# Four modulation blocks of the second layer computed between the layers, with the weights as the held operand

## The chip, the cores and the metric

The kernel runs on one core of one Trainium2 chip. The metric is the device time of one execution in microseconds; a lower time is better. Five engines work side by side, each through its own instructions in order, and wait for each other by semaphores: TensorE (PE, matrix products, with its weight loads listed apart as PEld), VectorE (DVE), ScalarE (ACT), GpSimd (POOL) and SyncE (SP, which here issues the transfers from and to DRAM).

## What is computed

A two-layer backbone over 512 latent tokens on an 8 x 64 grid and 256 context tokens, width 1024. Every sub-layer stands between a modulated RMS norm and a gated residual; shifts, scales and gates come from a small product of the conditioning vectors with a large matrix, per layer:

```python
for layer in range(DEPTH):
    mod_l = jnp.split((jax.nn.silu(c) @ w_mod[layer] + b_mod[layer])[:, None, :], 6, axis=-1)
    mod_c = jnp.split((jax.nn.silu(c_ctx) @ w_mod[layer] + b_mod[layer])[None, None, :], 6, axis=-1)
    hl = modulate(rmsnorm(xl, norm_g[layer, 0]), mod_l[0], mod_l[1])
    hc = modulate(rmsnorm(xc, norm_g[layer, 0]), mod_c[0], mod_c[1])
    ...  # layer 0: mLSTM and GLA heads; layer 1: RWKV-7 time mixing
    xl = xl + mod_l[2] * rmsnorm(yl, norm_g[layer, 1])
    hl = modulate(rmsnorm(xl, norm_g[layer, 2]), mod_l[3], mod_l[4])
    xl = xl + mod_l[5] * rmsnorm(conv_ffn(hl, ...), norm_g[layer, 3])
```

The change concerns `silu(c) @ w_mod[1]` and `silu(c_ctx) @ w_mod[1]`: two rows of 1024 times a matrix of 1024 x 6144. Only its first third (shift and scale of the first norm) is needed before the second layer's mixer; the gate `mod[2]` and what follows are needed after its recurrence.

## The kernel before, in words

Channels lie on partitions, eight groups of 128, tokens along the free axis: context first (256, `CTX`), then the latents (512, `LAT`), which the norms treat in two halves (`H0`, `H1`). Most products split float32 into a rounded high part and a low part: `unit` loads a raw weight tile `wraw` on SP, ACT casts it to `whi`, and POOL or DVE subtracts to get `wlo`; `dense` or `projn` then issues three matmuls for each piece. The raw tiles come from one ring of 15 buffers, and a load waits until the buffer's last reader has finished.

The matrix of modulations is cut into 12 blocks of 512 columns per layer. For the second layer, blocks 0 to 3 are done with split weights during the first layer. Blocks 4 to 11 are done by `mod_fill`: for each block four raw tiles `wfill` of 512 KB, unsplit; eight float32 matmuls in which the conditioning (`cth`, 128 x 2) is held and 512 weight columns move, giving 2 x 512 in one PSUM bank `mfill`; a copy into `frow`; four small matmuls with `sel` that turn the row into columns; and an addition of the bias into `modT`. Each float32 matmul is two instructions in the trace.

The second layer begins in `rwkv_mixer` with a stretch between the layers. The last pass of the first layer's down projection (`passes`, tile `po`) ends with the residual and the norm of each segment. `residual` squares the result (`xc`) and adds pairs; `rstd` sums over channels by matmuls against a column of ones (`rsb<-onek,xc`), takes the reciprocal root on POOL (`rsc`), spreads it by matmuls against the identity (`rsb<-ident,rsc`) and copies it; `normj` applies it to `y`. Then `enter` runs for the segment: `shift` (the difference to a neighbour on the grid, `xx`, mostly on POOL), and `variant` (the token mix, `vt`, its high part `vh` on ACT and its low part `vl` on DVE). Once the context is done the first four groups of the "v" projection begin (`first` and `projn`, PSUM tiles `pjC` for the context and `pjL` for the latents), with weights from `in_rkv`.

After that come low-rank projections, "r" and "k", and the recurrence in 16 units. Here a recording layer sets the order: `flow` takes generators (threads) and asks at each step which one could go on first by a table of costs (`Meter`); steps that need PSUM banks ask for them (`"@1"`). `mod_fill` is the last thread in that list and puts 7.0 of that clock between its matmuls. Outside `flow`, the order on each engine is the one that the program's list scheduler makes of the code.

Of the kernel before, what the change touches and what calls it, by code (L numbers as in the profile page):

```python
# [13 lines left out]
ALU = mybir.AluOpType  # L14
# [4 lines left out]
P = 128  # L19
# [8 lines left out]
LAT = (256, 512, "L", 0)  # L28
# [26 lines left out]
def chain(*gens):  # L55
    for g in gens:
        yield from g
# [7 lines left out]
def staggered(gens):  # L65

    live = []
    for g in gens:
        live = [h for h in live if next(h, drain) is not drain]
        live += [g] if next(g, drain) is not drain else []  # L70
    while live:
        live = [h for h in live if next(h, drain) is not drain]
# [10 lines left out]
def merge(*streams):  # L83


    st = [[g, tot, 0.0] for g, tot in streams]
    while st:
        stuck = True
        for e in sorted(st, key=lambda e: e[2] / e[1]):
            try:  # L90
                c = next(e[0])
            except StopIteration:
                st.remove(e)
                stuck = False
                break
            if c is not None:
                e[2] += c
                stuck = False
                break
        assert not stuck  # L100
# [117 lines left out]
def flow(meter, threads):  # L218

    done, waiting, ready, engine = {}, {}, [], {}
    for i, (name, g) in enumerate(threads):
        ready.append((0.0, i, name, g, 0))

    def place(g):
        while hasattr(g.gi_yieldfrom, "gi_frame"):
            g = g.gi_yieldfrom
        return g.gi_code.co_name, g.gi_frame.f_lineno if g.gi_frame else 0

    def when(e):

        return max(e[0], meter.free.get(engine.get(place(e[3])), 0.0)), not e[2].startswith("rec"), e[0], e[1]
    while ready:
        e = min(ready, key=when)
        ready.remove(e)
        t, i, name, g, n = e
        if n:
            b = meter.banks(n)
            if b is None:  # L240
                waiting.setdefault("@", []).append(e)
                continue
            if b > t:
                ready.append((b, i, name, g, n))
                continue
        meter.begin()
        at = place(g)
        x = next(g, None)
        engine[at] = meter.first
        ready += waiting.pop("@", ())  # L250
        t = max(t, meter.end if x is None or x is True else meter.head)
        if x is None:
            done[name] = t
            ready += [(max(t, t2), *r) for t2, *r in waiting.pop(name, ())]
        elif isinstance(x, str) and x[0] == "@":
            ready.append((t, i, name, g, int(x[1:])))
        elif isinstance(x, str):
            if x in done:
                ready.append((max(t, done[x]), i, name, g, 0))
            else:  # L260
                waiting.setdefault(x, []).append((t, i, name, g, 0))
        else:
            ready.append((t + (0.0 if isinstance(x, bool) else x), i, name, g, 0))
    assert not waiting, sorted(waiting)
# [10 lines left out]
DENSE = "g1 m0 t4 t5 v0 m1 t6 t7 m2 m3 t0 t1 t2 t3"  # L275
SPLIT_EARLY = (1, 2, 3)
MIXN = 12
MERGE = (197, 207.9, 39.4)
OUT_LAG = 7
POST_LAG = 0  # L280
# [5 lines left out]
class Net:  # L286
# [173 lines left out]
    def mod(self, layer, nb, lo=("pool",)):  # L460
        nc = self.nc
        ps = self.ps("R", name="modps")
        for kp in range(4):
            hi, w = self.unit(self.I["wmod"][layer, nb, kp], lo[(nb * 4 + kp) % len(lo)])
            for i in range(2):
                kc = 2 * kp + i
                nc.tensor.matmul(ps[0:4, :], self.c4[:, kc, :], hi[:, i * 512:(i + 1) * 512], start=kc == 0, stop=False)
                nc.tensor.matmul(ps[0:4, :], self.c4[:, kc, :], w[:, i * 512:(i + 1) * 512], start=False, stop=kc == 7)
        row = self.sl("mrow", 512)[0:4, :]
        nc.scalar.copy(row, ps[0:4, :])  # L470
        p2 = self.ps("R", name="modp2")
        for j in range(4):
            nc.tensor.matmul(p2[:, 2 * j:2 * j + 2], row[:, j * P:(j + 1) * P], self.sel, start=True, stop=True)
        b = self.v("bmod", layer * 48 + nb * 4, 4).unsqueeze(2).to_broadcast([P, 4, 2])
        nc.vector.tensor_tensor(self.modT[:, layer, nb * 4:nb * 4 + 4, :],
                                p2[:, 0:8].rearrange("p (j b) -> p j b", b=2), b, op=ALU.add)

    def mods(self, blocks):
        for layer, nb in blocks:
            self.mod(layer, nb)  # L480
            yield 3.4
# [479 lines left out]
    def even_mixer(self, mix, mh, ml, filler):  # L961
# [62 lines left out]
        def rec():  # L1024
            for c in heads():
                yield c
                if pend:
                    pend[0][0] -= 1
                    if pend[0][0] <= 0:
                        _, i, g = pend.pop(0)  # L1030
                        mix[i] = next(g)
                        yield 1.5
            for _, i, g in pend:
                mix[i] = next(g)
                yield 1.5
# [23 lines left out]
        dense = chain(*(part_of[n[0]](int(n[1:])) for n in DENSE.split()))  # L1059
        merge((dense, MERGE[0]), (rec(), MERGE[1]), (filler, MERGE[2]))  # L1060

# [180 lines left out]
    def rwkv_mixer(self, hf, xd, norms=None, post=lambda *a: None):  # L1242
        nc, I = self.nc, self.I
# [10 lines left out]
        def enter(j, seg):  # L1254
            self.shift(j, xx, hf, seg)
            yield
            yield from self.variant(3, j, xx, hf, vh, vl, seg[0], seg[0] + seg[1])
        for seg in (CTX, LAT):
            if norms is not None:
                next(norms)  # L1260
            staggered([enter(j, seg) for j in range(NC)])
        uw, ua, ug = self.sl("uw"), self.sl("ua"), self.sl("ug", LT)
        nc.gpsimd.memset(ua[64:128], 0.0)
        dv = self.dr.tile([P, NC, T], F32, name="dv")
# [66 lines left out]
        meter = self.nc = Meter(nc)  # L1331
# [10 lines left out]
        def kpart(p):  # L1342
            if p:
                yield f"kp{p - 1}"
            for x in keys:
                if x == "next":
                    return
                yield x
# [45 lines left out]
        def shared(p):  # L1394
            yield f"kp{p}"
            if p > 1:
                yield f"shared{p - 2}"
            yield from self.rwkv_shared(p, dv, dq, small, st[p])
# [12 lines left out]
        def close(p):  # L1411
            yield f"rec{2 * p + 1}"
            yield from self.rwkv_close(p, st[p], small, z_in if p >= 6 else lambda p, y: nc.sync.dma_start(dz[:, p, :], y))

        def z_in(p, z):
            zh[p], zl[p] = self.sl("zh", dt=F32R), self.sl("zl", dt=F32R)
            self.split(zh[p][:, CT:T], zl[p][:, CT:T], z)

        def early():
            yield "close5"  # L1420
            yield f"leaf{2 * NC - 1}"
            for p in range(6):
                z = self.sl("z", LT)
                meter.sync.dma_start(z, dz[:, p, :])
                z_in(p, z)
                yield False
            for m in range(NC):
                y.append(self.sl("y"))
                hi, lo = self.unit(I["rwo"][m, :, 0:6 * P], n=6 * P, lo="pool" if m % 2 else "dve")
                yield "@1"  # L1430
                ps = self.take("wo")
                for kc in range(6):
                    ks = slice(kc * P, (kc + 1) * P)
                    self.dense(hi[:, ks], lo[:, ks], zh, zl, kc, kc + 1, (LAT,), {"L": ps}, kc == 0, kc == 5)
                    yield False
                yield True
                meter.scalar.copy(y[m][:, CT:T], ps)
                self.close(ps)

        preps = [prep(u) for u in range(2 * NC)]  # L1440
        threads = [(f"kp{p}", kpart(p)) for p in range(NC)] + [(f"shared{p}", shared(p)) for p in range(NC)]
        for u in range(2 * NC):
            p, z = divmod(u, 2)
# [3 lines left out]
            threads += [(f"trans{g}_{u}", trans(u, g)) for g in ((0, 1, 2), (0, 2, 1))[z]]  # L1447
            threads += [(f"rec{u}", rec(u))]
            threads += [(f"close{p}", close(p))] if z else []
        flow(meter, threads + [("wo", early()), ("fill", self.mod_fill(1, range(4, 12)))])  # L1450
        self.nc = nc
        ss = self.sums(WO_SUMS)
        xc = self.rload(xd, CT)
# [452 lines left out]
    def run(self):  # L1906
# [27 lines left out]
        mh, ml = [None] * 8, [None] * 8  # L1934
        self.even_mixer(mix, mh, ml, self.mods(blocks[:MIXN]))
        B = self.coefB(0, 2, 1, "B01")
# [22 lines left out]
        def res2(seg, xc):  # L1959
# [9 lines left out]
            return norm  # L1969
        xc = self.ffn(0, hh, hl, THIRDS, y, ss, xd[0], res2, self.mods(blocks[MIXN:]))  # L1970

# [138 lines left out]
```

## Time and profile before

| | us |
|---|---|
| median of three runs | 2777.57 (2771.8 to 2782.0) |
| the profiled execution's own time | 2779.45 |
| its span in the profile | 2777.7 |
| its mean granted TensorE clock | 0.941 |
| busy: PE, PEld, DVE, ACT, POOL | 2531.4, 2051.6, 1563.7, 1055.1, 1069.2 |

All times of the trace are microseconds from the start of the span of that one execution. A row of the timeline has the start, the length, the engine, the line of the kernel, the operation with the tile it writes and the tiles it reads, and how many such stand together; in brackets the idle time of the engine before it and what ended that. For a matmul the shape of the held operand comes first (128*128), then that of the moving one (128x512). A row of the windows has a stretch, its length, each engine's busy time with the number of instructions, the granted TensorE clock as a share of full speed, the share of time in which the transfer engines were busy, and GB/s.

### The profile page before, as it was taken

Reading aid. Unit: us, or ns where it says so; the run is one execution under the profiler, and the core shown is the slowest. Engines: PE = TensorE matmul, PEld = TensorE weight load, DVE = VectorE, ACT = ScalarE, POOL = GpSimd, SP = SyncE. Lnnn points to the kernel's source line nnn. Section 1 sums busy time; section 2 is a strip of 40 time slices with the busy share of each in tenths; the row PEclk is TensorE's granted clock in tenths of the full one; section 3 lists DMA queues with packets and bytes.
Section 4 is the critical chain, followed back from the end, with each engine's and each line's share of the span. In section 5 each row is a group of like instructions: output and inputs, shape, how many; then the busy total and the mean of one; then the engine's idle time right before and its main releaser. Section 6 shows DMA issues by size and latency. Waiting matters only on the chain. (4 is left out here: it accounts for less than half of the span.)

```text
span 2777.7 us, 47275 instructions
## 1 busy us (share of the span) xinstructions
PE 2531.4 (91%) x19012; PEld 2051.6 (74%) x19012; DVE 1563.7 (56%) x2839; ACT 1055.1 (38%) x2205; POOL 1069.2 (38%) x1107
## 2 busy tenths in 40 slices
PE   5889999889989999987889979999999998989897
PEld 2677777768878888887767647577768777878786
DVE  4467856735555262647555374655566545675565
ACT  4543444444333132324343233334444444343232
POOL 2443445545333333336212251322232214455354
PEclk8999999989999999997999989999999998999998
DMA  6221234342121212132234454333322223222223
GB/s 225 72 82 54 76 120 139 112 144 90 41 69 49 74 41 74 54 121 77 89 105 140 155 138 87 82 91 99 83 51 63 46 75 125 78 92 95 71 81 107
DMA packets 195668, 254.58 MB, mean 92 GB/s; under 512 B 112120, under 2 KB 127864, under 8 KB 195448
## 3 DMA queue, kind: packets, MB, share of 16 engines
q1 hardware_dynamic: 195448, 251.56, 30.0%
q8 instruction: 149, 2.44, 0.4%
q14 instruction: 71, 0.58, 0.1%
HBM read 213.61 MB, written 37.89 MB: 91 GB/s over the span
## 5 line engine op out<-in xcount | busy, mean ns | idle before, releaser
L377 POOL TENSOR_TENSOR wlo<-wraw,whi 128x512 fp32r<-128x512 f32 (+1 forms) x469 | 640.6, 1383 | 848.2 <-ACT whi L376 741.4
L1101 DVE SCALAR_TENSOR_TENSOR fa<-pl,vec,fa 128x512 f32<-128x512 f32 x352 | 361.3, 1040 | 265.9 <-ACT fa L1098 258.5
L376 ACT CAST whi<-wraw 128x512 fp32r<-128x512 f32 (+1 forms) x529 | 297.7, 599 | 464.6 <-DMA wraw<-in_up 185.1
L214 POOL TENSOR_SCALAR_AFFINE_SELECT T<-T 64x256 f32<-64x256 f32 x192 | 100.6, 526 | 264.7 <-ACT T L214 211.6
L388 PE MATMUL pdL<-gh,whi 128*128 128x512 f32 x288 | 117.9, 409 | 19.6 <-DVE y L1160 11.4
L389 PE MATMUL pdL<-gl,whi 128*128 128x512 f32 x288 | 117.0, 406 | 8.3 <-POOL gl L1121 8.3
L388 PE MATMUL pjL<-mh,whi 128*128 128x512 f32 x304 | 120.3, 396 | 1.5 <-DVE fa L1104 1.5
L389 PE MATMUL pjL<-ml,whi 128*128 128x512 f32 x304 | 120.6, 397 | 0.0
L392 PE MATMUL pjL<-mh,wlo 128*128 128x512 f32 x304 | 120.2, 395 | 0.0
L389 PE MATMUL pjL<-zl,whi 128*128 128x512 f32 x304 | 119.6, 393 | 0.0
L392 PE MATMUL pjL<-zh,wlo 128*128 128x512 f32 x304 | 119.5, 393 | 0.0
L388 PE MATMUL pjL<-zh,whi 128*128 128x512 f32 x304 | 119.5, 393 | 0.0
L392 PE MATMUL pdL<-gh,wlo 128*128 128x512 f32 x288 | 116.6, 405 | 0.0
L214 DVE TENSOR_SCALAR SU<-cst,el 64x64 f32<-64x64 f32 x176 | 51.1, 291 | 111.1 <-PE cst L214 107.8
L1102 ACT ACTIVATE fa<-fa 128x256 f32<-128x256 f32 (+1 forms) x66 | 36.9, 560 | 188.7 <-DVE fa L1101 188.7
L388 PE MATMUL pjC<-mh,whi 128*128 128x256 f32 x304 | 85.8, 282 | 8.7 <-DVE fa L1104 8.7
L214 ACT ACTIVATE SU<-cst,el 64x64 f32<-64x64 f32 x176 | 53.7, 308 | 100.5 <-PE cst L214 100.1
L1160 DVE TENSOR_TENSOR y<-y,pdL 128x512 f32<-128x512 f32 x48 | 32.5, 687 | 105.1 <-PE pdL L392 105.1
L214 PE MATMUL pmy<-T,q0t 64*64 64x192 f32 x768 | 90.4, 341 | 0.8 <-DVE SU L214 0.8
L214 PE MATMUL ps<-bk,av 64*64 64x192 f32 x768 | 87.8, 350 | 3.5 <-DVE bk L214 2.0
L389 PE MATMUL pjC<-ml,whi 128*128 128x256 f32 x304 | 85.4, 281 | 0.0
L392 PE MATMUL pjC<-mh,wlo 128*128 128x256 f32 x304 | 85.1, 280 | 0.0
(501 smaller groups left out, 7275.8 us busy)
## 6 DMA issues: line engine op xcount, KB each, us to landing
wraw<-in_up SPq DMA_DIRECT2D x88, 512.0 KB, 3.7
wraw<-in_wmod SPq DMA_DIRECT2D x64, 512.0 KB, 3.9
wfill<-in_wmod SPq DMA_DIRECT2D x32, 512.0 KB, 5.0
wraw<-in_rkv SPq DMA_DIRECT2D x24, 512.0 KB, 4.1
wraw<-in_win_fm SPq DMA_DIRECT2D x21, 512.0 KB, 4.2
wraw<-in_down SPq DMA_DIRECT2D x32, 320.0 KB, 2.9
xd<-y SPq DMA_DIRECT2D x64, 128.0 KB, 1.8
wraw<-in_down SPq DMA_DIRECT2D x32, 256.0 KB, 2.7
```

What stands on the lines that cost most here:

```text
L214: return f(*a, **k)
L376: nc.scalar.copy(hi[:, c], raw[:, c])
L377: (nc.gpsimd if lo == "pool" else nc.vector).tensor_tensor(w[:, c], raw[:, c], hi[:, c].bitcast(F32), op=ALU.subtract)
L388: nc.tensor.matmul(pst[tag][:m, :w], w1, xh[kc][:, o:o + w], start=st, stop=False)
L389: nc.tensor.matmul(pst[tag][:m, :w], w1, xl[kc][:, o:o + w], start=False, stop=False)
L392: nc.tensor.matmul(pst[tag][:m, :w], w0, xh[kc][:, o:o + w], start=False, stop=sp)
L1101: nc.vector.scalar_tensor_tensor(b, src, fw(f, i), b, op0=ALU.mult, op1=ALU.add)
L1102: nc.scalar.activation(a, a, AF.Gelu_apprx_tanh)
L1160: nc.vector.tensor_tensor(yj, yj, pst[tag][:, :w], op=ALU.add)
```

## The change

Blocks 4 to 7 leave the fill of the recurrence, which keeps 8 to 11. A new function `mod_idle` does them, called four times right after the latents' `enter` loop. It loads the same four tiles of 512 KB per block (named `wmod`), but holds a 128 x 128 piece of the weights in the array and moves the conditioning (128 x 2) past it: 32 float32 matmuls per block, which accumulate into eight columns of one PSUM bank `modps`. The result has its columns on partitions already, so that the copy and the four `sel` matmuls fall away, and the addition of the bias follows at once.

```diff
--- before.py
+++ after.py
@@ -275,6 +275,7 @@
 DENSE = "g1 m0 t4 t5 v0 m1 t6 t7 m2 m3 t0 t1 t2 t3"
 SPLIT_EARLY = (1, 2, 3)
 MIXN = 12
+IDLE_MODS = (4, 5, 6, 7)
 MERGE = (197, 207.9, 39.4)
 OUT_LAG = 7
 POST_LAG = 0
@@ -474,6 +475,22 @@
         b = self.v("bmod", layer * 48 + nb * 4, 4).unsqueeze(2).to_broadcast([P, 4, 2])
         nc.vector.tensor_tensor(self.modT[:, layer, nb * 4:nb * 4 + 4, :],
                                 p2[:, 0:8].rearrange("p (j b) -> p j b", b=2), b, op=ALU.add)
+
+    def mod_idle(self, layer, nb):
+
+        nc = self.nc
+        ps = self.ps("R", name="modps")
+        for kp in range(4):
+            w = self.rt("wmod")
+            nc.sync.dma_start(w, self.I["wmod"][layer, nb, kp])
+            for i in range(2):
+                for j in range(4):
+                    kc = 2 * kp + i
+                    nc.tensor.matmul(ps[:, 2 * j:2 * j + 2], w[:, i * 512 + j * P:i * 512 + (j + 1) * P], self.c2[:, kc, :],
+                                     start=kc + j == 0, stop=kc == 7 and j == 3)
+        b = self.v("bmod", layer * 48 + nb * 4, 4).unsqueeze(2).to_broadcast([P, 4, 2])
+        nc.vector.tensor_tensor(self.modT[:, layer, nb * 4:nb * 4 + 4, :],
+                                ps[:, 0:8].rearrange("p (j b) -> p j b", b=2), b, op=ALU.add)
 
     def mods(self, blocks):
         for layer, nb in blocks:
@@ -1259,6 +1276,8 @@
             if norms is not None:
                 next(norms)
             staggered([enter(j, seg) for j in range(NC)])
+            for nb in ((), IDLE_MODS)[seg is LAT]:
+                self.mod_idle(1, nb)
         uw, ua, ug = self.sl("uw"), self.sl("ua"), self.sl("ug", LT)
         nc.gpsimd.memset(ua[64:128], 0.0)
         dv = self.dr.tile([P, NC, T], F32, name="dv")
@@ -1447,7 +1466,7 @@
             threads += [(f"trans{g}_{u}", trans(u, g)) for g in ((0, 1, 2), (0, 2, 1))[z]]
             threads += [(f"rec{u}", rec(u))]
             threads += [(f"close{p}", close(p))] if z else []
-        flow(meter, threads + [("wo", early()), ("fill", self.mod_fill(1, range(4, 12)))])
+        flow(meter, threads + [("wo", early()), ("fill", self.mod_fill(1, range(4 + len(IDLE_MODS), 12)))])
         self.nc = nc
         ss = self.sums(WO_SUMS)
         xc = self.rload(xd, CT)
```

The order on PE between the layers, before: a piece of the context's "v" projection (`pjC`, from `vh` and `vl`) with the last of four sums of the last latent half (`rsb<-onek,xc`) and its identity matmul.

```order
6035 L414 MATMUL pjC_10991<-vh_10770,whi_10961 128x256
6036 L415 MATMUL pjC_10991<-vl_10778,whi_10961 128x256
6037 L416 MATMUL pjC_10991<-vh_10770,wlo_10962 128x256
6038 L535 MATMUL rsb_10873<-onek_80,xc_10132 128x1 x2
6039 L414 MATMUL pjC_10992<-vh_10770,whi_10969 128x256
6040 L415 MATMUL pjC_10992<-vl_10778,whi_10969 128x256
6041 L416 MATMUL pjC_10992<-vh_10770,wlo_10970 128x256
6042 L414 MATMUL pjC_10993<-vh_10770,whi_10977 128x256
6043 L541 MATMUL rsb_10873<-ident_74,rsc_10882 128x128 x2
6044 L415 MATMUL pjC_10993<-vl_10778,whi_10977 128x256
```

After: the same place in the program, the second to fourth sums of the same `rsb`.

```order
5957 L552 MATMUL rsb_10873<-onek_80,xc_10128 128x1 x2
5958 L415 MATMUL pjC_11159<-vh_10763,whi_11129 128x256
5959 L416 MATMUL pjC_11159<-vl_10771,whi_11129 128x256
5960 L489 MATMUL modps_11037<-cth_87,wmod_11038 128x2 x8
5961 L489 MATMUL modps_11037<-cth_87,wmod_11048 128x2 x8
5962 L489 MATMUL modps_11037<-cth_87,wmod_11058 128x2 x6
5963 L552 MATMUL rsb_10873<-onek_80,xc_10130 128x1 x2
5964 L489 MATMUL modps_11037<-cth_87,wmod_11058 128x2 x2
5965 L489 MATMUL modps_11037<-cth_87,wmod_11068 128x2 x8
5966 L489 MATMUL modps_11079<-cth_87,wmod_11080 128x2 x8
5967 L489 MATMUL modps_11079<-cth_87,wmod_11090 128x2 x8
5968 L489 MATMUL modps_11079<-cth_87,wmod_11100 128x2 x8
```

The 128 calls of `modps` (64 of them in the rows shown, 64 between the first two sums: a row ahead of these) stand between the first and the fourth sum of the last latent half, and `pjC` has only begun; before, the products with all four weights (`pjC` 10991 to 10994) were under way there.

The loads and the splitting of the "v" weights, on SP and on POOL. SP, before: the last weights of the down projection, the first four "v" weights (`in_rkv`), and the residual's stores (`xd`).

```order
106 L370 DMA wraw<-in_down 128x2x512 x4
107 L370 DMA wraw<-in_rkv 128x1024 x4
108 L603 DMA xd_95<-y 128x256 x8
109 L370 DMA wraw<-in_rkv 128x1024
110 L603 DMA xd_95<-y 128x256 x8
111 L370 DMA wraw<-in_rw 128x1024
112 L370 DMA wraw<-in_rkv 128x1024
```

SP, after:

```order
106 L371 DMA wraw<-in_down 128x2x512 x4
107 L485 DMA wmod<-in_wmod 128x1024 x7
108 L620 DMA xd_95<-y 128x256 x8
109 L485 DMA wmod<-in_wmod 128x1024 x3
110 L620 DMA xd_95<-y 128x256 x5
111 L485 DMA wmod<-in_wmod 128x1024
112 L620 DMA xd_95<-y 128x256 x3
113 L485 DMA wmod<-in_wmod 128x1024 x4
114 L620 DMA xd_95<-y 128x256 x2
115 L485 DMA wmod<-in_wmod 128x1024
116 L620 DMA xd_95<-y 128x256
117 L371 DMA wraw<-in_rkv 128x1024
```

The new loads (`wmod`) have taken the places of the "v" weights, of which the first now stands behind all sixteen and behind all but five of the stores.

POOL, before: low halves of the "v" weights (`wlo`), the last pair sum `xc`, the reciprocal root `rsc`, and the latents' grid shift (`xx`, 128x8x63).

```order
172 L377 TENSOR_TENSOR wlo<-wraw,whi 128x512
173 L610 TENSOR_TENSOR xc<-xc 128x256
174 L601 TENSOR_TENSOR y<-y,xc 128x256
175 L1183 TENSOR_TENSOR xx<-y 128x255 x2
176 L601 TENSOR_TENSOR y<-y,xc 128x256
177 L539 TENSOR_TENSOR rsc<-rsc,powc 128x2
178 L1183 TENSOR_TENSOR xx<-y 128x8x63 x4
```

POOL, after:

```order
166 L627 TENSOR_TENSOR xc<-xc 128x256
167 L618 TENSOR_TENSOR y<-y,xc 128x256
168 L1200 TENSOR_TENSOR xx<-y 128x255
169 L618 TENSOR_TENSOR y<-y,xc 128x256
170 L556 TENSOR_TENSOR rsc<-rsc,powc 128x2
171 L378 TENSOR_TENSOR wlo<-wraw,whi 128x512
172 L1200 TENSOR_TENSOR xx<-y 128x8x63 x4
173 L1200 TENSOR_TENSOR xx<-y 128x448 x4
174 L378 TENSOR_TENSOR wlo<-wraw,whi 128x512
```

The low halves that stood among the context's shift have moved behind the root, all but one of them behind the latents' shift.

In the recurrence, on PE, before: a piece with the fill's `mfill` between `pmg`, `pmy`, `cst` and others.

```order
7432 L214 MATMUL ps_16815<-ri,bk 64x128 x8
7433 L214 MATMUL ps_16816<-ri,bk 64x128 x8
7434 L214 MATMUL mfill<-wfill,cth 2x512
7435 L214 MATMUL pmg<-q0t,T_16183 64x64 x8
7436 L214 MATMUL pmy<-T_16183,q0t 64x192 x8
7437 L214 MATMUL pln<-blk,lsq 128x2 x4
7438 L214 MATMUL cst<-SU,bm 64x64 x2
7439 L214 MATMUL mfill<-wfill,cth 2x512
7440 L214 MATMUL cst<-SU,bm 64x64 x2
```

After, in the same part of the recurrence:

```order
7445 L214 MATMUL pmg<-W,T_16129 64x64 x8
7446 L214 MATMUL pmg<-q0t,T_16130 64x64 x8
7447 L214 MATMUL pmy<-T_16130,q0t 64x192 x8
7448 L214 MATMUL pmg<-T_16129,J 64x128 x8
7449 L214 MATMUL pmg<-W,T_16131 64x64 x8
7450 L214 MATMUL cst<-SU,mgl 64x64 x2
7451 L214 MATMUL pln<-blk,lsq 128x2 x4
7452 L214 MATMUL pmt<-bm,T_16129 128x64 x2
```

No `mfill` stands there any more: the fill's four remaining blocks are placed as the first four were before, and end early in the recurrence.

## Prediction

> **What bounds the kernel now.** I read the page's first part, then the windows of the two stretches that the change touches, the instructions of TensorE (PE) in time there, and the chain of waits inside the recurrence.
>
> ```profile
> span 2777.7 us, 47275 instructions
> PE 2531.4 (91%) x19012; PEld 2051.6 (74%) x19012; DVE 1563.7 (56%) x2839; ACT 1055.1 (38%) x2205; POOL 1069.2 (38%) x1107
> ```
>
> PE is the bound over the whole, but the average hides two very different places. First the stretch between the layers. The columns are the stretch, its length, busy time and instructions of PE, of PE's weight loads, of DVE, ACT and POOL, then the granted TensorE clock, the DMA share and GB/s:
>
> ```profile
> 1279.40:1303.30 23.90, 16.70 (x68) 15.23 (x69) 19.46 (x44) 12.57 (x31) 15.79 (x18) 0.50 0.28 89
> 1303.30:1317.00 13.70, 10.79 (x86) 10.04 (x84) 8.97 (x22) 4.17 (x11) 6.54 (x9) 1.00 0.26 78
> 1317.00:1330.60 13.60, 3.64 (x9) 2.71 (x10) 13.60 (x17) 4.98 (x10) 9.44 (x9) 0.50 0.00 0
> 1330.60:1350.00 19.40, 19.40 (x85) 15.77 (x84) 6.06 (x12) 4.79 (x12) 0.00 (x0) 1.00 0.00 1
> ```
>
> Here PE waits: it is busy for 31 of the 51 us from 1279.4 to 1330.6, and the clock stands at half in two of the three windows. What it waits for is a chain through every engine, in order of time:
>
> ```profile
> 1298.43 0.84 POOL L610 TENSOR_TENSOR xc<-xc 128x256 f32<-128x256 f32 x1
> 1299.33 1.01 PE L535 MATMUL rsb<-onek,xc 128*128 128x1 f32 x4 [1.53 <-POOL xc L610]
> 1312.47 0.61 PE L535 MATMUL rsb<-onek,xc 128*128 128x1 f32 x4
> 1314.12 0.71 PE L541 MATMUL rsb<-ident,rsc 128*128 128x128 f32 x4 [0.46 <-POOL rsc L539]
> 1314.91 0.37 ACT L545 COPY rsb<-rsb 128x256 f32<-128x256 f32 x1 [2.95 <-PE rsb L541]
> 1315.32 7.21 DVE L570 SCALAR_TENSOR_TENSOR y<-y,A,rsb 128x256 f32<-128x256 f32 x8 [2.04 <-ACT rsb L545]
> 1316.42 9.29 POOL L1183 TENSOR_TENSOR xx<-y 128x504 f32<-128x504 f32 x8 [2.36 <-ACT y L572]
> 1326.29 1.95 ACT L1216 CAST vh<-vt 128x512 fp32r<-128x512 f32 x3 [3.23 <-DVE vt L1215]
> 1326.96 0.79 PE L414 MATMUL pjL<-vh,whi 128*128 128x512 f32 x1 [11.54 <-ACT vh L1216]
> ```
>
> The squares of the last latent half (xc) are summed by four groups of matmuls against a column of ones, the first at 1299.33; the reciprocal root is spread by the identity (rsb<-ident, 1314.12); norm, grid shift and token mix follow on DVE, ACT and POOL; and the latent "v" projection (pjL) can start only then, at 1326.96. Whatever delays the identity matmul delays everything behind it. Idle PE time after it is not free for work that stands ahead of it.
>
> Second the recurrence, where the fill stands now; the next three rows are mfill's instructions alone (without POOL), and the last is the chain of waits of the first stretch, by line:
>
> ```profile
> 1738.00:2094.00 356.00, 339.33 (x4396) 246.55 (x4396) 213.73 (x593) 143.52 (x346) 103.86 (x202) 0.96 0.33 81
> 2094.00:2303.00 209.00, 200.76 (x2855) 163.50 (x2852) 113.96 (x317) 86.31 (x215) 44.66 (x78) 0.95 0.25 63
> 1440.00:1738.00 298.00, 32.69 (x82) 5.89 (x82) 0.50 (x3) 1.73 (x3) 0.91 0.45 130
> 1738.00:2094.00 356.00, 41.96 (x110) 7.91 (x110) 0.80 (x5) 2.88 (x5) 0.96 0.33 81
> sum 863.00, PE 74.64 PEld 13.81 DVE 1.30 ACT 4.60; mean PE 24.88 PEld 4.60 DVE 0.43 ACT 1.53
> by line: PE ps L214 15.0%; PE pmg L214 13.5%; PE cst L214 9.1%; PE pmt L214 9.0%; PE mfill L214 8.6%; PE pmy L214 6.7%; DVE leaf L214 6.0%; PE pw L214 4.4%; issue 3.0%; PE yps L214 2.5%; DVE mgl L214 2.3%; DVE L L214 2.2%; DVE SU L214 1.9%;
> ```
>
> PE is busy 95% of it at nearly full clock, so there removed PE time comes back.
>
> **The change part by part.**
>
> *What the recurrence gives back.* Eight blocks cost 74.64 us of PE, 9.33 each, so four cost 37.3. Not all of it was on the path: in 1738 to 2094 mfill holds 8.6% of the chain, 30.6 of its 41.96 us, which is 73%; 73% of 37.3 is 27. Against that, each of these blocks held one PSUM bank and sixteen DMAs of 512 KB leave the queue that also carries the recurrence's own tiles, so other waits may shorten. I take 31, between chain (27) and PE time (37). As bounds I keep 20 (dependences on DVE, 60% busy there, take over more) and 42 (banks and queue help besides).
>
> *What the new blocks cost on PE.* 4 x 32 = 128 matmuls of float32, each two instructions in the trace, as are the present fill's (64 calls, x128 below): 256 instructions, each with its own 128x128 weights and two moving columns. The kernel has the same shape already, the pn matmuls:
>
> ```profile
> L214 PE MATMUL mfill<-wfill,cth x128: 591/592/1061, 1466.3 to 2062.9; 128*2 128x512 f32 x128
> 1566.60 2.74 PE L214 MATMUL pn<-blk,ksq 128*128 128x2 f32 x24
> 1569.20 0.48 PE L214 MATMUL pk<-vh,whi 128*128 128x512 f32 x1
> 2341.97 3.55 PE L535 MATMUL rsb<-onek,ss 128*128 128x1 f32 x16
> 2345.39 2.70 PE L535 MATMUL rsb<-onek,xc 128*128 128x1 f32 x12
> ```
>
> 24 pn from 1566.60 to 1569.20 are 0.108 us each at the full clock. 16 rsb from 2341.97 to 2345.39 are 0.214 each at the half clock. So 256 instructions take 27.7 us or 54.8 us, and the granted clock decides which:
>
> ```profile
> 1562.60:1566.10 3.50, 3.50 (x17) 2.13 (x16) 0.08 (x1) 2.33 (x4) 0.00 (x0) 1.00 0.22 80
> 1566.10:1569.50 3.40, 3.40 (x30) 3.33 (x29) 0.30 (x2) 0.01 (x1) 1.22 (x1) 1.00 0.03 5
> 1569.50:1573.00 3.50, 3.50 (x13) 3.00 (x12) 0.04 (x1) 0.00 (x0) 3.28 (x2) 0.51 0.00 0
> 2341.00:2347.80 6.80, 6.71 (x32) 6.71 (x32) 4.70 (x9) 2.33 (x7) 2.43 (x4) 0.50 0.79 258
> ```
>
> The second window is full of pn, PE busy without a gap, and the clock is halved right behind it, in the third. In the fourth, 32 matmuls of one column stand back to back for 6.7 us and the clock stays at half throughout. So a stream of matmuls that load weights and move one or two columns doesn't raise the clock here, however busy PE looks, and a raised clock falls under it. The new blocks begin at about 1298, in a window at 0.50 (first row of the stretch above). I take 54.8.
>
> The Trainium skill ("TensorE: Matmul & The Clock Gate", Part 1) says that the gate goes to full rate after about 3.4 us of sustained PE busyness, and that it is time that counts, not the number of matmuls. Read literally it would have the new blocks at full rate after their first window, 28 to 30 us in all; the two windows quoted speak against that reading for this shape.
>
> *Where they stand.* In the order of the changed program all 256 stand between the first and the last xc group of the last latent half, so ahead of its identity matmul. First xc group to identity took 1314.12 - 1299.33 = 14.8 us before, with 86 short matmuls of the context "v" projection (pjC) between. Now the stretch holds the 54.8 us, four xc groups (four instructions at 0.214 each, 3.4 us together), 13 pjC (a 512-column matmul at the full clock is 19.40 / 85 = 0.228 us from the fourth window of the stretch, so 256 columns at half clock cost as much: 3.0) and about 1 us for the root and its way to PE: 62 us. The first xc group comes a little earlier, since POOL no longer splits the first "v" weights ahead of its xc sum:
>
> ```profile
> 1294.06 1.28 POOL L377 TENSOR_TENSOR wlo<-wraw,whi 128x512 fp32r<-128x512 f32 x1 [3.00 <-ACT whi L376]
> 1296.17 1.46 POOL L377 TENSOR_TENSOR wlo<-wraw,whi 128x512 fp32r<-128x512 f32 x1
> 1225.75 15.52 SPq L370 DMA_DIRECT2D wraw<-in_rkv  x4
> ```
>
> These two are 2.7 us on POOL, so I let it start 1 to 2 us earlier, at about 1298. The identity then ends its wait at about 1360: 45 us late.
>
> *What moves behind it.* Before, 90 of 96 pjC stood ahead of the identity; now 13 do, and 77 follow, 77 x 0.114 = 8.8 us. The 11.54 us in which PE waited for vh would hide them, but 46 of them use the third and fourth "v" weights and stand behind the first pjL. Those weights are late: four buffers' loads were issued from 1225.75 on, about 58 us ahead of the first use; now the raw tiles take buffers that the new weights hold, loaded earlier on the same queue, and come free only as the new matmuls finish. Their low halves stand on POOL behind the grid shift (9.29 us, eight instructions) and on DVE behind most of the latent token mix, in a stretch where DVE is busy 13.60 of 13.60 us. So 46 x 0.114 = 5.2 us of pjC, plus a low half or two at 1.3 to 1.5, go onto the path: 7 us (bounds 1 and 13). The new DMAs themselves are hidden: seven of the sixteen stand behind no buffer that is in use after the down projections, long ahead of 1298, and 512 KB each at the 258 GB/s of the row at 2341 is 2.0 us, against 16 matmuls x 0.214 = 3.4 us that use it. The four additions into modT are 0.17 us each on DVE and wait for PE; behind the first three stands one xc sum that the last xc group needs, and it is ready before the fourth block ends. They cost nothing while the blocks are this slow.
>
> The loss is 45 + 7 = 52 us (46 to 58). Sum: 52 - 31 = +21. Against the profiled execution's 2779.45 that is 2800; it lies 1.9 above the median of the three runs (2777.57), so I predict 2798 for the median. The bounds make it 2778 + 46 - 42 = 2782 at one end and 2778 + 58 - 20 = 2816 at the other. A measurement of this kernel can tell about 0.5%, 14 us, from no change.
>
> **The rivals.**
>
> *The clock rises (not slower).* If the new blocks count as activity, as the skill's rule read literally has it, they take 3.4 us at the half rate (16 instructions) and 240 x 0.108 = 26 us after it, 29 us in all; pjC and the xc groups run at the full rate too. The loss falls to about 26, and 26 - 31 = -5: 2773. For it: PE is gapless in that stretch, and the window at 1303.30 had the full clock. Against it: that window's PE time was mostly pjC with 256 columns, and the rows at 1566 and 2341. It decides from the point where the loss is 45, i.e. where about a quarter of the stream runs at the full clock; then the kernel is not slower by what can be told.
>
> *The recurrence gives little back.* Its chain also has DVE and issue in it (leaf 6.0%, issue 3.0%, mgl, L, SU). If the fill mostly stood in gaps that dependences leave, four blocks return 15 or less: 52 - 15 = +37, 2815. For it: the fill yields between its matmuls to everything else. Against: 73% of it is on the chain.
>
> *The recurrence gives back more than PE time.* With a bank free throughout and fewer transfers, 42 returned: +10, 2788. For it: eight banks serve all threads and a fill block holds one for some 75 us (eight between 1466.3 and 2062.9). Against: the stretch from 2094 on has no fill, and PE is busy there by the same share (200.76 / 209 = 0.96, against 339.33 / 356 = 0.95), so banks were not what held it.
>
> **How the numbers follow.** Slower by 52 - 31: 0.64, its own range 2785 to 2808. Clock rises: 0.12, at 2773. Little back: 0.13, at 2815. More back: 0.11, at 2788. The range 2778 to 2816 leaves out most of the clock's case and little else. Faster by over 0.5% (below 2764) needs a raised clock and a full return together: 0.06. Within 0.5% (2764 to 2791): the rest of the clock's case, most of "more back", and the low end of the likeliest: 0.30. Slower: 0.64.
>
> **What would show it.** Granted clock 0.50 from about 1298 to 1357 with modps instructions 0.21 us apart; rsb<-ident of the last latent half at 1360 instead of 1314; the fourth window's pjL ending at about 1402 instead of 1350; then, against this shift of 52, the end of the recurrence (2303 before) only some 21 later. Wrong would be: modps 0.11 apart; a shift after the projection far from 52 because the late "v" weights cost more or nothing; a recurrence whose length shrinks by less than 20 or more than 42.

## Result, and the profile after

The changed kernel takes 2807.36 us (median of four runs, 2803.4 to 2815.22), against 2774.69 for the kernel before (four runs, 2769.29 to 2782.0). The ratio is 1.0109, 95% interval 1.0089 to 1.013: slower by 30 us (25 to 36; the medians lie 33 apart). The forecast was 21 slower.

The page of the profiled execution, whose own time is 2815.22:

```profile
span 2813.4 us, 47590 instructions
PE 2560.3 (91%) x19172; PEld 2107.8 (75%) x19172; DVE 1566.7 (56%) x2839; ACT 1051.8 (37%) x2201; POOL 1069.8 (38%) x1107
```

PE is busy for the same 91%, and busy 29 us longer: the shares tell nothing of what happened. The windows between the layers do (columns as before):

```profile
1230.00:1296.50 66.50, 54.13 (x392) 52.54 (x390) 38.84 (x96) 25.98 (x66) 32.64 (x44) 0.83 0.48 163
1296.50:1357.50 61.00, 60.95 (x285) 60.95 (x286) 11.10 (x33) 4.76 (x12) 5.22 (x8) 0.50 0.26 71
1357.50:1371.80 14.30, 4.43 (x29) 4.01 (x27) 12.74 (x14) 5.45 (x12) 10.86 (x9) 0.74 0.04 14
1371.80:1416.90 45.10, 43.65 (x219) 37.31 (x220) 17.34 (x29) 18.29 (x37) 13.70 (x10) 0.91 0.26 88
```

The second row is the new work: 61 us in which PE has no gap, its weight loads (second pair) have none either, the granted clock is 0.50 to the end, and DVE, ACT and POOL have little to do (11, 5 and 5 us). The third row is the old wait ahead of the latent projection, moved but not filled. The same in time, with the first low-rank matmul (prL), which comes behind the first four groups of the "v" projection, and in the last row that of before:

```profile
1296.56 1.01 PE L552 MATMUL rsb<-onek,xc 128*128 128x1 f32 x4 [7.73 <-POOL xc L627]
1297.43 27.45 PE L489 MATMUL modps<-cth,wmod 128*128 128x2 f32 x128
1326.16 9.38 PE L489 MATMUL modps<-cth,wmod 128*128 128x2 f32 x44
1336.25 18.06 PE L489 MATMUL modps<-cth,wmod 128*128 128x2 f32 x84
1357.52 1.05 PE L558 MATMUL rsb<-ident,rsc 128*128 128x128 f32 x4
1371.87 1.22 PE L415 MATMUL pjL<-vh,whi 128*128 128x512 f32 x2 [9.28 <-ACT vh L1233]
1416.75 0.44 PE L389 MATMUL prL<-rh,whi 128*128 128x512 f32 x1
...
1361.92 0.39 PE L388 MATMUL prL<-rh,whi 128*128 128x512 f32 x1
```

128 instructions in 27.45 us, 0.214 each, and 256 in 54.9. The identity comes at 1357.5 (1314.1 before), pjL at 1371.9 (1327.0), prL at 1416.75 (1361.92).

Such marks can't be taken from the span's start alone. The last matmul of the down projection, ahead of everything that changed on the computing engines, starts at a different time in each execution, though PE, DVE, ACT and POOL do the same in the same order up to there:

```profile
1229.23 0.39 PE L392 MATMUL pdL<-gh,wlo 128*128 128x512 f32 x1
...
1234.18 0.39 PE L393 MATMUL pdL<-gh,wlo 128*128 128x512 f32 x1
...
1217.24 0.40 PE L393 MATMUL pdL<-gh,wlo 128*128 128x512 f32 x1
```

These are before, after, and one of the experiments below (late64). So the loss is read from this pdL to prL, between which the same matmuls stand in both kernels, but for modps: 132.7 us before, 182.6 after, 50 us lost. This mark has a scatter too: in the kernels below that have nothing new in this place (drop2, drop4, drop8) it is 137.4, 132.2 and 132.9 us.

And the recurrence, from the first to the last yps (its reads of the state), before and after:

```profile
1736.70:2302.70 566.00, 541.09 (x7276) 411.03 (x7274) 328.59 (x913) 230.43 (x563) 148.55 (x280) 0.96 0.30 74
...
1786.50:2340.40 553.90, 517.41 (x7182) 413.78 (x7178) 330.81 (x909) 226.90 (x559) 147.41 (x277) 0.92 0.27 61
```

It is 12 us shorter, though the fill has left nearly all of it. PE is less busy (517 of 554 us, 0.93, where it was 0.96), and the granted clock fell from 0.96 to 0.92. Both are what the experiments had to explain.

### The profile page after: what moved, and what is told of

The parts are those of the page before. It is cut to its first block, busy times and chain, and to the rows that moved or that the text cites. A ratio compares the mean times of both kernels' runs of the same rounds, so it can differ in the third digit from the quotient of the medians.

```text
span 2813.4 us, 47590 instructions
## 1 busy us (share of the span) xinstructions
PE 2560.3 (91%) x19172; PEld 2107.8 (75%) x19172; DVE 1566.7 (56%) x2839; ACT 1051.8 (37%) x2201; POOL 1069.8 (38%) x1107
## 5 line engine op out<-in xcount | busy, mean ns | idle before, releaser
L214 PE MATMUL ps<-bk,av 64*64 64x192 f32 x768 | 93.7, 363 | 3.2 <-DVE bk L214 1.6
```

The lines of the kernel that those rows point to most:

```text
L214: return f(*a, **k)
```

## Experiments

"Clock theory" is this: the fill's 512 moving columns kept the granted clock up in the recurrence, and its removal let the clock fall; in the same way the new blocks' two moving columns keep it down between the layers. "Dependence theory" is the rival: the recurrence waits on other engines once PE has less to do, and the clock only follows. Half clock time, where it is named, is the time for which the granted clock stood at half (in these traces it is only ever half or full).

**The return alone: drop2, drop4, drop8.** From the changed kernel, or the same with two or eight blocks in the tuple. The products of these blocks are left out, and only the bias goes into modT:

```diff
             for nb in ((), IDLE_MODS)[seg is LAT]:
-                self.mod_idle(1, nb)
+                nc.vector.tensor_copy(self.modT[:, 1, nb * 4:nb * 4 + 4, :], self.v("bmod", 48 + nb * 4, 4).unsqueeze(2).to_broadcast([P, 4, 2]))
```

> Blocks 4 to 7 are left out altogether (only the bias is written into modT), the fill keeps blocks 8 to 11: the changed kernel without its new work, so the recurrence's return alone. If the return is what the prediction took (31 us): 2744 us against a before of about 2775. If it is what the marks of the two traces suggest (the recurrence ends 37.7 us late after a projection that ended 54.8 us late, so 17 us): about 2757. Clock theory: time at the half clock from the first yps to the last rises from 48 us to some 80 to 90 as in the changed kernel, since the fill's wide moves kept the clock up. Dependence theory: PE's idle time there rises, and the clock's time does not matter.

> All eight fill blocks are left out (bias only): how the return goes on. By PE time alone eight blocks give 62 to 75 us: 2700 to 2713. Clock theory: the second four return little, since even more windows fall to the half clock (over 100 us of it between the first yps and the last): 2740 to 2755. Dependence theory: also little, with PE idle growing by some 25 us but the half clock time not much above 85.

> Blocks 4 and 5 left out altogether (bias only), the fill keeps six blocks: the recurrence's return for two blocks without any new work. It has the same order in the recurrence as the kernel with two blocks between the layers, which came out 17.5 us below before. If its gain is the recurrence's return, this one is at 2750 to 2756 (a return of 15 to 20 for two blocks, as much as four give, because the clock holds with six blocks of fill: some 50 us at the half clock between the first and the last yps). If the return is 4.7 us per block as four and eight dropped blocks gave: 2761 to 2766, and the other kernel's gain came also from elsewhere.

| blocks left out | ratio to before | 95% interval | us returned |
|---|---|---|---|
| 2 | 0.9945 | 0.9927 to 0.9962 | 15 |
| 4 | 0.9933 | 0.9907 to 0.996 | 19 |
| 8 | 0.9857 | 0.9829 to 0.9886 | 40 |

Four blocks return 19 us (11 to 26), not 31: the term that was wrong, without any of the new work. Half clock time between first and last yps was 85 us, as in the changed kernel, and 48 before. Eight return 40, some 5 us per block as with four, half of a block's PE time. For eight the clock theory was a miss in the time (20 to 35 returned) and in its cause: half clock time was 79 us there, where over 100 were expected. The dependence theory was a miss in the time too, though half clock time is not much above 85 us there, as it had said. Two blocks return 15, the lower end of what was expected if the clock holds (half clock time 61 us, where some 50 were expected); the interval (10 to 20) all but reaches 5 per block.

**What moves past the weights, in the recurrence: held2, held64.** From the kernel before; both have the fill's matmuls replaced by

```diff
-                    nc.tensor.matmul(ps[0:2, :], self.c2[:, 2 * kp + i, :], ws[kp][:, i * 512:(i + 1) * 512], ...)
+                    for j in range(4):
+                        nc.tensor.matmul(ps[:, 2 * r * j:2 * r * j + 2 * r], ws[kp][:, i * 512 + j * P:i * 512 + (j + 1) * P],
+                                         self.c2[:, 2 * kp + i, :].unsqueeze(1).to_broadcast([P, r, 2]), ...)
```

with r = 1 or 32, without frow and sel, and with the planner's cost of such a call set to 0.22.

> The kernel before, with all eight fill blocks kept in the recurrence but done as in the new function: weights held (128x128), 2 columns moving, no frow and sel steps; 512 instructions, at 0.108 us each 55 us of PE where the fill had 75. Clock theory: nothing of the fill raises the clock any more, so half clock time in the recurrence is 85 us or more, and it is no faster than before (2770 to 2800), slower than its twin with 64 moving columns by 10 us or more. Dependence theory: faster than before by up to 20 us, and the same as its twin within 4 us.

> Twin of the one with 2 moving columns: the same held weights, with the conditioning's two columns repeated 32 times (64 moving columns), the same number of instructions. Clock theory: the moved columns count, half clock time in the recurrence is near that of before (about 50 us), and it is 10 us or more faster than the twin: 2750 to 2775. Dependence theory: as the twin, within 4 us.

held2 took 1.0131 of before (1.0097 to 1.0165), held64 1.0023 (0.9999 to 1.0047). Medians 2813.26 and 2778.94: 34 us (30 by the ratios) between twins with the same number of instructions, whose orders differ for a few hundred of them, where one moves 2 columns and the other 64. held2 came out slower still than was expected (2770 to 2800). The windows from first to last yps, held2 first:

```profile
1730.10:2345.20 615.10, 586.46 (x7527) 471.80 (x7525) 334.12 (x912) 228.51 (x561) 146.40 (x283) 0.89 0.29 70
...
1716.70:2304.80 588.10, 556.21 (x7527) 450.25 (x7525) 336.02 (x912) 227.59 (x561) 146.51 (x283) 0.94 0.30 73
```

The same 7527 matmuls, PE busy 586 against 556 us, clock 0.89 against 0.94 (half clock time 137 against 72 us). PE is 0.95 busy in both (idle 29 and 32 us): it isn't that one waits more, the same work runs slower. This is the clock theory's effect, made by the moved columns, unless the differences of order count for something. That held64 is no faster than before was a small miss of the upper end.

**The new work alone: both8.** The changed kernel with `range(4, 12)` put back in the fill, so that blocks 4 to 7 are done twice.

> The changed kernel with the fill's eight blocks all kept as well, so blocks 4 to 7 are computed twice: the cost of the new blocks alone. The marks say 54.8 us up to the end of the first v projection; if nothing of it is taken back later: before + 55 = 2830. If part is taken back later (from there to the first yps 5 us came back in the changed kernel, of which a part may be the fill's): 2822 to 2830. Together with the kernel that only drops the four blocks, the two differences should add up to the change (+33) if the parts don't touch each other.

1.015 (1.0129 to 1.0172): 42 us lost (36 to 48), less than expected. From the last pdL to prL it is 178.4 us, 46 more than before, close to the changed kernel's 50. With the 19 returned by drop4 the parts give +23, with an uncertainty of some 9; the change is +30.

**What moves past the weights, between the layers: late2, late64, late128.** Three kernels with one order on PE. All new blocks wait for the first normalised latent group, since they read a copy of the conditioning made behind it; 2, 64 or 128 columns move.

```diff
+            if seg is LAT:
+                self.cl = tp.tile([P, NC, 2], F32, name="cl")
+                nc.vector.scalar_tensor_tensor(self.cl..., hf[0][:, T - 16:T], 0.0, self.c2..., op0=ALU.mult, op1=ALU.add)
             for nb in ((), IDLE_MODS)[seg is LAT]:
                 self.mod_idle(1, nb)
```

> The changed kernel with the new blocks made to wait for the first normalised latent channel group (they read a copy of the conditioning, which one DVE instruction makes behind it): all 256 stand behind the identity matmul of the last latent half, 2 columns moving as before. Place theory: the norm chain is not late any more, the 12 us gap ahead of the first pjL hides a part; the stream still runs at 0.21 us each, 55 us, so the first v projection ends 55 - 12 = 43 us late instead of 55: about 2796, 10 to 14 us less than the changed kernel. If the chain was not what made the loss: no difference.

> The same as the kernel with the blocks behind the identity and 2 columns, in the same order of instructions, but with the conditioning's columns repeated to 64 moving columns. Clock theory: after the first window (3.4 us) the granted clock is 1.00, the 256 instructions take 0.11 to 0.13 us each, 30 to 34 us, and the time is some 20 to 25 us less than its twin: about 2773. If the moved columns don't set the clock: the same as its twin or slower, 2796.

> Third twin of the two kernels whose new blocks stand behind the identity matmul, in the same order on PE, with 128 moving columns instead of 2 or 64. Those two ran all 256 instructions at the half clock (0.214 us each, 54.8 us in all). If moved columns per time raise the clock and 64 were too few: the first 16 or so at 0.21, the rest at 0.11 to 0.12 us, 30 to 33 us in all, and the time some 22 to 25 us less, about 2787. If what made the kernel with 128 columns in the first place fast was its order (96 calls behind the identity) and not its clock: 0.21 to 0.24 us each and 2811 again.

The 256 instructions in the timelines of the three, in this order:

```profile
1317.76 54.75 PE L489 MATMUL modps<-cl,wmod 128*128 128x2 f32 x256 [19.49 <-issue]
...
1311.33 54.85 PE L489 MATMUL modps<-cl,wmod 128*128 128x64 f32 x256 [19.48 <-issue]
...
1313.40 31.06 PE L489 MATMUL modps<-cl,wmod 128*128 128x128 f32 x256 [19.51 <-issue]
```

and the windows of late64 and, from its fourth microsecond, of late128:

```profile
1311.40:1366.10 54.70, 54.70 (x257) 54.70 (x258) 4.98 (x11) 6.59 (x12) 4.97 (x4) 0.50 0.22 71
...
1317.00:1344.40 27.40, 27.40 (x242) 27.40 (x242) 5.21 (x10) 6.83 (x12) 5.95 (x5) 0.98 0.46 141
```

PE is busy without a gap in both. With 64 columns the clock stays at 0.50 for 54.7 us; with 128 it is up after some 5 us, and the stream takes 31 us (of which 4.8 would be at 0.214 us per instruction and 26.3 at 0.1125, which wide128 below shows at the full clock). The expectation for 64 was a miss of the dose, not of the cause. Ratios: late2 1.0126 (1.0096 to 1.0157), late64 1.0111 (1.008 to 1.0141), late128 1.0083 (1.006 to 1.0105). The 24 us of the stream show in full up to prL (late64 194.4 us from pdL, late128 168.1). In the medians, 2811.52 and 2792.42, it is 19; by the ratios, whose intervals overlap, it is 8.

late2 was also the test of the place, and there the expectation failed: no gain over the changed kernel. The identity was early (1297), but the copy was made only at 1317.50, 20 us behind it (it stands behind most of the latent token mix in DVE's order), so that the 12 us gap was over before the stream began. And the "v" weights load into buffers that the new weights hold, so that their splitting waits for the stream. The waits of its twin late64 between 1280 and 1420 (engine and line, what it waited for, us in total, times, longest) show that:

```profile
ACT whi L377 <- PE modps L489: 29.5, 4, 9.4
```

pdL to prL took 193.7 us in late2, more than in the changed kernel. So late2 doesn't show what the gap would have hidden had the stream begun right behind the identity.

**128 columns in the first place: wide128.** The changed kernel with

```diff
-                    nc.tensor.matmul(ps[:, 2 * j:2 * j + 2], w[...], self.c2[:, kc, :], ...)
+                    nc.tensor.matmul(ps[:, 128 * j:128 * j + 128], w[...], self.c2[:, kc, :].unsqueeze(1).to_broadcast([P, 64, 2]), ...)
```

The addition of the bias reads two of each 128 columns.

> The changed kernel with 128 moving columns (the conditioning's two repeated 64 times), no other edit. Its order differs: 32 of the 128 calls stand ahead of the identity matmul, 96 behind it (with 2 columns it was all 128 ahead). Clock theory: instructions at about 0.12 us once the clock is up, the identity 8 to 14 us late instead of 44, the first v projection 25 to 32 us late: 2775 to 2785. Otherwise, with the clock at half, 128 columns at 0.21 to 0.25 us and the projection 45 to 55 us late: 2800.

0.9955 of before (0.9938 to 0.9973), median 2763.23: this one is faster than before, and than was expected (2775 to 2785). Its timeline:

```profile
1288.07 3.51 PE L489 MATMUL modps<-cth,wmod 128*128 128x128 f32 x16
1292.34 3.59 PE L489 MATMUL modps<-cth,wmod 128*128 128x128 f32 x30
...
1299.48 0.71 PE L559 MATMUL rsb<-ident,rsc 128*128 128x128 f32 x4 [0.55 <-POOL rsc L557]
1300.03 21.60 PE L489 MATMUL modps<-cth,wmod 128*128 128x128 f32 x192
...
1372.27 0.40 PE L389 MATMUL prL<-rh,whi 128*128 128x512 f32 x1
```

The first 16 instructions take 0.22 us each, the last 192 take 0.1125. These stand behind the identity, and the identity is not late (72.2 us behind pdL, 84.9 before), where 8 to 14 us late were expected; from pdL to prL it is 145.0 us, 12 more than before, where 25 to 32 were expected. Two things differ from the changed kernel here, clock and order, since the list scheduler places wider calls later; late64 against late128 shows the clock's part with the order held.

**Two blocks: two128.** The same with `IDLE_MODS = (4, 5)`.

> Only blocks 4 and 5 between the layers, with 128 moving columns; the recurrence keeps six. 128 instructions, 3.4 us at half clock and 12.6 at full: 16 us, of which the wait ahead of the first pjL (11.5) hides most and the chain's own gaps some: 0 to 5 us of loss. The return is half of what dropping four blocks gave (18.6): 9. Together 2766 to 2770, between the kernel before (2774) and the one with four blocks (2763).

0.9936 (0.9921 to 0.9951), median 2753.51, the fastest of those that do all of the work: 18 us below before (14 to 22). That was a miss (2766 to 2770 were expected), since the return of two blocks had been taken as 9. From pdL to prL it is 134.1 us, within what the kernels with nothing new there show (132.2 to 137.4), so the new work is hidden in the chain's gaps and the wait ahead of pjL as far as this mark can tell. Nearly all of the gain is the return that drop2 shows (15).

**Spreading the fill: spread20.** wide128 with `yield 20.0` for `yield 7.0` in the fill.

> The kernel with 128 moving columns and one more edit: the four remaining fill blocks of the recurrence put 20 instead of 7 of the planner's microseconds between their matmuls, so that they reach into its second half rather than end near its first unit. The work is the same. Clock theory: wide moves in more of the windows, less time at the half clock between the first and the last yps than the 65 us of its parent, and 4 to 10 us faster: 2753 to 2759. Dependence theory: as its parent, 2763 within 4 us.

0.9976 (0.9958 to 0.9995), median 2765.48. Half clock time was 65 us in both: spreading four blocks doesn't hold the clock up, and nothing was gained. A miss for the clock theory's remedy; the dependence theory's number (2763 within 4) was met.

**The recurrence of one program in six executions.** Changed kernel, drop4, wide128, late2, late64 and late128 have the very same order on PE from the first fill instruction on. From first to last yps, in this order without the first, which stands above, and in the last row both8, which has the order of before with all eight blocks:

```profile
1725.50:2277.10 551.60, 515.15 (x7180) 411.75 (x7178) 330.29 (x907) 227.12 (x559) 146.09 (x277) 0.92 0.26 61
...
1745.00:2289.50 544.50, 508.34 (x7180) 408.54 (x7178) 331.85 (x907) 226.75 (x559) 147.86 (x277) 0.94 0.27 62
...
1791.20:2338.10 546.90, 510.51 (x7182) 409.24 (x7178) 331.07 (x905) 227.04 (x559) 148.40 (x277) 0.93 0.27 62
...
1784.70:2338.20 553.50, 518.75 (x7180) 414.54 (x7178) 330.39 (x907) 226.68 (x559) 145.87 (x277) 0.92 0.26 61
...
1758.80:2315.90 557.10, 522.02 (x7182) 416.72 (x7178) 330.35 (x908) 227.44 (x559) 147.73 (x277) 0.91 0.26 60
...
1769.50:2342.30 572.80, 549.25 (x7276) 416.84 (x7274) 328.57 (x909) 230.45 (x563) 147.81 (x280) 0.94 0.29 73
```

With four blocks, length and clock go together: 544.5 us at 0.94, 557.1 at 0.91 (half clock time 65 and 99 us), 0.37 us of length for each us of half clock time. both8 had 68 us of half clock time; the four-block program took 544.5 us at 65 and 546.9 at 72 (late2), so some 27 less than both8's 572.8. So at an equal clock the return is about what the chain of waits had said (27).

What becomes of the rest can be read from PE. Its idle time in this stretch (the length less its busy time) goes with the program and not with the clock: 24.9 and 23.6 us with eight blocks (before and both8), 34.8 to 36.5 in all six with four. (It doesn't go on growing: drop8, in yet another order, has 33.) Its busy time without the fill goes with the clock: 499 us in before (half clock time 48), 504 in wide128 (65), 507 in both8 (68), 513 in the changed kernel (85), 518 in late128 (99). Of the 37.7 us of PE time that mfill loses in this stretch between before and the changed kernel (41.96 less 4.26), 12 came back, 12 became idle time and 14 went into the other matmuls, which took longer. So each theory has a part of it: PE waits more for other engines, as the dependence theory says, and the clock costs time of its own.

How much the clock falls for want of the fill can't be read from single traces, since 48 and 68 us stand against 65 to 99. The granted clock of all executions says more: its mean is 0.9405 in 13 of before (0.936 to 0.944) and 0.9355 in the four of drop4 taken with them (0.933 to 0.938). That is some 25 us more of half clock time in an execution, or 9 us at 0.37 for each, and 27 less 9 is 18, against the 19 that drop4 returned. With two blocks left out the mean doesn't fall (0.941, and 0.941 for before beside it), and with eight it falls no further (0.937). That a lower clock makes these executions longer, and not the other way round, rests on executions that differed by chance; held2 and held64 are the case in which the moved columns were what was changed.

## Why the prediction came out as it did

**Right: the shape runs at the half clock.** 0.214 us per instruction and 54.9 in all, against 54.8. The rival in which the clock rises is ruled out for 2 columns, and shown for 128. The Trainium skill ("TensorE: Matmul & The Clock Gate", Part 1) has the gate open after about 3.4 us of sustained busyness, counted in time; the 54.7 us of late64, PE without a gap and the clock at 0.50, don't agree with that for matmuls that move 64 columns or fewer over new weights each time, and late128 agrees.

**Right: how long the norm chain waits, with luck in the marks.** From the first xc group to the identity it took 61.0 us, foreseen 62. That pjL came 44.9 later than before, as foreseen (45), is luck: 5 us of it lie ahead of the change (pdL at 1234.18 instead of 1229.23). From pdL, the identity is 38 later and pjL 40.

**Nearly right: what follows and what leads.** From pjL to prL it took 44.9 us instead of 35.0, so 10 rather than 7. The start came earlier than the 1 to 2 us taken: from the last pdL to the first xc group 62.4 us instead of 70.1, so 8 earlier. The low halves of the "v" weights were off POOL in all of that stretch, and POOL is busy 32.3 us in it instead of 40.3; that this is the reason is likely, not shown. The two misses offset each other: 50 us lost, foreseen 52.

**Wrong in size: what the recurrence gives back.** 19 us (11 to 26) where 31 was taken and 20 was the lower bound. From prL to the last yps it shrank by 17 us (940.6 to 923.5), less than the 20 under which the prediction called itself wrong. The step that failed is "PE is busy 95% of it at nearly full clock, so there removed PE time comes back". The chain's share of 73% was right: it leaves 10 of four blocks' 37 us unreturned, and PE's idle time grew by 12. But the clock was read as a property of the stretch. In part it was the work of the fill, whose matmuls move 512 columns among the recurrence's with 64 to 192: without four blocks it is lower, which took back some 9 us by the mean of the executions and 14 in the profiled pair. Going up from the chain's 27 to 31, for banks and queue, found no support. The rival "the recurrence gives little back" came nearer in price (15), and its reason, gaps that dependences leave, is one half of what was lost; it doesn't explain held2 against held64. How the return goes with the number of blocks (15, 19, 40 for two, four, eight) is not explained by a clock that falls more with each, since it doesn't, and stays open.

The net, +30, lies in the likeliest case's range (2785 to 2808 for 2777.57, so +7 to +30) at its upper end.

## What to carry to other kernels

Before a stream of small matmuls is moved, look in the trace for a stretch of the same shape and at the clock granted in and behind it: its price can differ by two, and wide operands that look wasteful may pay for themselves through the clock of their neighbours. Work taken out of a stretch with a high clock may have been part of what held it up, and PE may only wait more without it: its PE time was an upper bound of the return here (19 of 37 us for four blocks). When work is put ahead of a chain that other engines wait for, count first how much fits in that chain's gaps: with 128 columns two blocks did here, four did not.

## What the runs showed of the hardware

A gapless stream of float32 matmuls, each with its own 128x128 weights, stays at the half clock for 55 us with 2 or 64 moving columns, at 0.214 us per instruction; with 128 the clock is up within some 5 us and an instruction then takes 0.1125 us. So moving 64 times as many columns made the same stream 1.8 times as fast (54.8 against 31.1 us). Two executions had come to the same instruction, by the same instructions in the same order, 17 us apart (1217.24 and 1234.18, after 99 and 126 us of half clock time). That is more than most terms here: marks are to be taken from a point just ahead of the change.
